# One of SyncE's three closing stores, split into four transfers over the DMA engines

## The chip, the cores and the metric

The kernel runs on one core of a Trainium2 chip. The metric is the device time of one execution in microseconds. Beside each timed kernel stands one profiled execution, whose trace gives the profile. A store or load is cut into rows, one row for each partition, and the rows are dealt out to the core's 16 DMA engines.

## The reference

The kernel computes the product of attention weights and values for 8 x 12 = 96 heads, all in float32:

```python
batch, n_heads, seq, head_dim = 8, 12, 1024, 64
np.einsum('bhqs,bhsd->bhqd', attn_weights, v)
```

The weights are 96 matrices of 1024 x 1024 (403 MB), v and the output 96 matrices of 1024 x 64 (25 MB each).

## The kernel before, in words

The heads are taken four at a time: NV = 24 groups q of four heads, each worked in two units, so NU = 48 units n. One unit's weights are loaded by GpSimd in one transfer (`load_attn`, lines 362 to 368), cast to bf16 on the way, into one of two buffers `abf`. TensorE transposes them in blocks against an identity (line 146), VectorE and ScalarE copy the transposed blocks from PSUM to `at` (line 302), TensorE multiplies them with the group's values `vbf` (line 207), the product goes to `ot` (line 310), is transposed back (line 192) and copied by ScalarE to the output buffer `osb` (line 283; the last unit's copy is shared with VectorE, line 343).

`osb` has five slots of two groups each; `slot(q)` gives the slot of group q. Two groups make 2 MB, 16 KiB in each of 128 partitions. Outputs are not stored when they are ready, but in bursts, since `osb` holds ten groups:

- behind the load for unit 18 GpSimd stores groups 0 to 7, behind that for unit 34 groups 8 and 9 and then 10 to 13 (`BURSTS`, lines 64 and 428 to 430);
- at the end of its program GpSimd stores groups 14 and 15, then 16 and 17 (lines 431 to 433; `HELD_FROM` = 14, `BY_SYNC` = 18), with `single_packet`;
- SyncE (SP) stores groups 18 and 19, then 20 and 21 (lines 458 and 459), and last 22 and 23 (lines 460 and 461).

What sets SP's order is its own program, lines 440 to 463. It passes on the landings of loads to TensorE (lines 445 to 456). The weights of the last two units (`HALVED` = 46 and on) come in two halves each, and line 455 waits for the second half of each. Only then does SP wait for the bursts (line 457, long true by then) and come to its stores, so that the first two are issued right behind the landing of the last load. `store` (lines 376 to 382) waits on `s_out`, which counts ScalarE's copies to `osb`, and issues one DMA that adds 16 to the semaphore `s_end` when it has landed, one from each DMA engine. The last store waits for the last copies through `s_vbf` (line 460).

The end of the program is ScalarE's wait on `s_end` (line 464) for the value that line 463 has put in a register: 16 for each of SP's stores, so 48. GpSimd's two last stores are waited for in line 357.

Of the kernel before, what the change touches and what calls it, by code (L numbers as in the profile page):

```python
# [10 lines left out]
def kernel(  # L11
# [18 lines left out]
    nc = tc.nc  # L30
# [5 lines left out]
    D = v.shape[-1]  # L36
    NH = B * H
    P = 128
    VH = 4
    VP = P // VH  # L40
    G = Q // VP // 2
# [8 lines left out]
    NV = NH // VH  # L50
# [4 lines left out]
    BY_SYNC = NV - 6  # L55
# [12 lines left out]
    def slot(q):  # L68
        return q % NO // 2
# [4 lines left out]
    def out_n(q, fours):  # L74
        return out_h[ds(q * VH, fours * VH)].rearrange(
            "(n eight) (p r) d -> (eight p) n (r d)", eight=V8, p=P // V8
        )
# [24 lines left out]
    osb = sb("osb", [P, NO // 2, 4 * G, D], fp32)  # L102
# [10 lines left out]
    s_v, s_osb, s_end, s_second = sem("s_v"), sem("s_osb"), sem("s_end"), sem("s_second")  # L113

    s_bank = [sem(f"s_bank{b}") for b in range(4)]
    s_ot, s_vbf, s_out = sem("s_ot"), sem("s_vbf"), sem("s_out")
# [21 lines left out]
    with tc.tile_critical(sync_engine=mybir.EngineType.Pool, no_gpsimd_drain=True):  # L138
# [237 lines left out]
        def store(q, fours, eng, done, ready=None):  # L376
            eng.wait_ge(s_out, ready or 2 * (q + fours) + 1)
            at_slot = osb[:, ds(slot(q), fours // 2)].rearrange("p n r d -> p n (r d)")
            eng.dma_start(  # L379
                out=out_n(q, fours), in_=at_slot,  # L380
                **({"single_packet": True} if eng is pool and fours == 2 else {}),
            ).then_inc(done, 16)

        def store_2(q):
            store(q, 2, pool, s_osb)

# [6 lines left out]
            out=ident,  # L393
            in_=ident,
# [8 lines left out]
            out=spread,  # L403
            in_=spread,
# [8 lines left out]
            out=spread_4,  # L413
            in_=spread_4,
# [6 lines left out]
        for n in range(NU - 2):  # L421
            q, i = n // 2, n % 2
# [9 lines left out]
        for q in range(HELD_FROM, BY_SYNC, 2):  # L432
            store_2(q)
# [11 lines left out]
        for k in range(1, NV // 2):  # L445
            stored = 2 * (k - 1)
            if stored in BURSTS:
                done = list(BURSTS).index(stored)
# [6 lines left out]
            nc.sync.wait_ge(*second_of(n))  # L455
            nc.sync.sem_inc(s_half)
        nc.sync.wait_ge(s_osb, 16 * sum(len(x) for x in BURSTS.values()))
        for q in range(BY_SYNC, NV - 2, 2):
            store(q, 2, nc.sync, s_end)
        nc.sync.wait_ge(s_vbf, NV * VH + 2)  # L460
        store(NV - 2, 2, nc.sync, s_end, NU)
        landed = nc.scalar.alloc_register("landed")
        nc.scalar.reg_mov(landed, 16 * (NV - BY_SYNC) // 2)
    tc.keep_in_program_order(nc.scalar.wait_ge(s_end, nc.scalar.snap(landed)))
    tc.keep_in_program_order(nc.scalar.sem_inc(s_end, 1))

# [29 lines left out]
```

## Time and profile before

| | |
|---|---|
| median of 3 runs | 1051.45 us (1051.25 to 1051.61) |
| the profiled execution | 1051.77 us |
| its span, first to last instruction | 1050.0 us |
| mean granted TensorE clock | 0.874 |
| TensorE busy | 792.7 us (75%) |
| VectorE / ScalarE busy | 389.9 us (37%) / 469.5 us (45%) |
| DMA packets and bytes moved | 10662, 239.68 MB |
| read from HBM / written to it | 427.82 MB / 25.17 MB |
| SP's stores issued at | 1024.9, 1025.3 and 1037.7 us |

Times in the trace are counted from the span's first instruction. "DMA" rows give the mean busy share of the 16 DMA engines in tenths, 9 for 90% or more, and GB/s what they moved, with a packet's bytes counted in the slice where it starts; in a window the 40 slices are as long as the window divided by 40. A queue's line gives its packets, megabytes, and the time that its packets took as a share of the time of 16 engines. q0 is GpSimd's queue of transfers, q1 SP's. Packets under 512 bytes are the completions by which a DMA engine tells that its share of a transfer is done, or other small ones. The packets carry no number of the DMA engine that moved them.

### The profile page before, as it was taken

Reading aid. Unit: us, or ns where it says so; the run is one execution under the profiler, and the core shown is the slowest. Engines: PE = TensorE matmul, PEld = TensorE weight load, DVE = VectorE, ACT = ScalarE, POOL = GpSimd, SP = SyncE. Lnnn points to the kernel's source line nnn. Section 1 sums busy time; section 2 is a strip of 40 time slices with the busy share of each in tenths; the row PEclk is TensorE's granted clock in tenths of the full one; section 3 lists DMA queues with packets and bytes.
Section 4 is the critical chain, followed back from the end, with each engine's and each line's share of the span. In section 5 each row is a group of like instructions: output and inputs, shape, how many; then the busy total and the mean of one; then the engine's idle time right before and its main releaser. Section 6 shows DMA issues by size and latency. Waiting matters only on the chain.

```text
span 1050.0 us, 17671 instructions
## 1 busy us (share of the span) xinstructions
PE 792.7 (75%) x7272; PEld 708.0 (67%) x7272; DVE 389.9 (37%) x585; ACT 469.5 (45%) x590; POOL 38.1 (4%) x69
## 2 busy tenths in 40 slices
PE   0777789489789493887949879859578794988984
PEld 0676678478678482777848678747567684878874
DVE  1443344235334251343424344324224341533542
ACT  0445355345445361344535455344335443545643
POOL 2000000000000000000000000000000000000100
PEclk9889789799898796889879989889879987889997
DMA  9999999999999999999999999999999999999998
GB/s 216 224 220 217 218 218 206 220 220 220 216 220 215 212 216 379 220 216 218 211 216 217 220 220 216 209 225 216 324 227 218 219 208 225 216 213 220 213 222 384
DMA packets 10662, 239.68 MB, mean 228 GB/s; under 512 B 1056, under 2 KB 1056, under 8 KB 1184
## 3 DMA queue, kind: packets, MB, share of 16 engines
q0 software_dynamic: 10080, 232.26, 98.8%
q1 hardware_dynamic: 576, 7.34, 1.7%
q8 instruction: 3, 0.05, 0.0%
q14 instruction: 3, 0.02, 0.0%
HBM read 427.82 MB, written 25.17 MB: 431 GB/s over the span
## 4 chain that ended last, share of the span: by engine, by line
DMA 71%; PE 26%; issue 1%; POOL 1%; ACT 0%; DVE 0%; ACTq 0%; SPq 0%; POOLq 0%
DMA abf<-in_attn_weights_dram 63%; PE bank L146 22%; DMA out_dram<-osb 8%; PE bank L163 2%; PE bank L207 1%; PE bank L192 0%; POOL vr L371 0%; ACT osb L283 0%; DVE osb L283 0%; ACT vbf L275 0%; PE bank L179 0%; POOL abf L365 0%; ACT ot L310 0%; POOL out_dram L379 0%; ACTq L283 0%
## 5 line engine op out<-in xcount | busy, mean ns | idle before, releaser
L146 PE MATMUL bank<-ident,abf 128*128 128x128 f32 x3072 | 432.3, 308 | 207.7 <-DMA abf<-in_attn_weights_dram 184.6
L146 PEld LDWEIGHTS bank<-ident,abf 128*128 128x128 f32 x3072 | 422.6, 212 | 219.3 <-DMA abf<-in_attn_weights_dram 192.1
L302 DVE COPY at<-bank 128x1024 bf16<-128x1024 bf16 x480 | 319.7, 688 | 399.7 <-PE bank L146 397.6
L302 ACT COPY at<-bank 128x1024 bf16<-128x1024 bf16 x288 | 287.9, 1012 | 327.2 <-PE bank L146 327.2
L207 PE MATMUL bank<-at,vbf 128*64 128x256 bf16 x3072 | 224.8, 285 | 0.0
L207 PEld LDWEIGHTS bank<-at,vbf 128*64 128x64 bf16 x3072 | 203.6, 111 | 20.1 <-issue 11.2
L283 ACT COPY osb<-bank 64x512 f32 (+1 forms) x194 | 112.4, 580 | 32.9 <-PE bank L192 30.3
L310 DVE COPY ot<-bank 128x512 f32<-128x512 f32 x48 | 33.2, 691 | 210.0 <-PE bank L207 210.0
L192 PE MATMUL bank<-ident,ot 128*128 128x128 f32 x392 | 61.3, 308 | 34.5 <-ACT vbf L275 26.3
L310 ACT COPY ot<-bank 128x512 f32<-128x512 f32 x48 | 28.1, 585 | 130.5 <-PE bank L207 130.5
L192 PEld LDWEIGHTS bank<-ident,ot 128*128 128x128 f32 x392 | 50.4, 157 | 46.6 <-ACT vbf L275 37.1
L163 PE MATMUL bank<-vr,spread 32*128 32x512 bf16 x704 | 79.8, 375 | 1.3 <-issue 0.9
L163 PEld LDWEIGHTS bank<-vr,spread 32*128 32x128 bf16 x704 | 32.7, 93 | 41.2 <-issue 4.1
L275 ACT CAST vbf<-bank 128x512 bf16<-128x512 f32 x48 | 25.8, 588 | 70.9 <-PE bank L163 69.5
L365 POOL DMA_DIRECT2D abf<-in_attn_weights_dram x50 | 26.9, 537 | 811.6 <-PE bank L146 810.8
L275 DVE CAST vbf<-bank 128x512 bf16<-128x512 f32 x48 | 30.9, 686 | 28.8 <-PE bank L163 28.0
L302 ACT ACT_TABLE_LOAD x12 | 15.4, 1283 | 6.1 <-DMA osb<-in_v_dram 5.9
L371 POOL DMA_DIRECT2D vr<-in_v_dram x6 | 4.0, 674 | 134.1 <-PE bank L163 112.6
L379 POOL DMA_DIRECT2D out_dram<-osb x5 | 3.1, 620 | 7.7 <-ACT osb L283 7.7
L283 DVE COPY osb<-bank 64x512 f32<-64x512 f32 x2 | 1.4, 690 | 3.0 <-PE bank L192 3.0
L345 DVE MEMSET ident<- 128x128 f32 x1 | 0.2, 165 | 5.9 <-DMA osb<-in_v_dram 5.9
L179 PE MATMUL bank<-vr,spread 32*128 32x512 bf16 x32 | 2.1, 377 | 0.1
(13 smaller groups left out, 9.9 us busy)
## 6 DMA issues: line engine op xcount, KB each, us to landing
abf<-in_attn_weights_dram POOLq DMA_DIRECT2D x46, 4096.0 KB, 29.1
vr<-in_v_dram POOLq DMA_DIRECT2D x5, 2048.0 KB, 15.2
out_dram<-osb POOLq DMA_DIRECT2D x1, 8192.0 KB, 40.2
abf<-in_attn_weights_dram POOLq DMA_DIRECT2D x4, 2048.0 KB, 24.6
out_dram<-osb POOLq DMA_DIRECT2D x3, 2048.0 KB, 35.4
out_dram<-osb SPq DMA_DIRECT2D x3, 2048.0 KB, 13.5
out_dram<-osb POOLq DMA_DIRECT2D x1, 4096.0 KB, 42.4
osb<-in_v_dram SPq DMA_DIRECT2D x1, 1024.0 KB, 4.8
```

What stands on the lines that cost most here:

```text
L146: last = pe.matmul(out=pt[g % 4][:, k], lhsT=words[:, k], rhs=ident, is_transpose=True, start=(k == 0), stop=(k == KW - 1),)
L163: last = pe.matmul(out=banks[h], lhsT=spread[rows, j, ds(VB - 1 - b, P)], rhs=vr[rows, n // 2, b], start=(b == 0), stop=(b == VB - 1),)
L179: last = pe.matmul(out=banks[h], lhsT=spread_4[rows, h, ds(VF - 1 - b, P)], rhs=vr[rows, 0, n * VF + b], start=(b == 0), stop=(b == VF - 1),)
L192: last = pe.matmul(out=px[j0 // 4][:, ds(j * P, P)], lhsT=ot[:, j0 + j], rhs=ident, is_transpose=True, start=(j == 0), stop=(j == 3),)
L207: last = pe.matmul(out=outs, lhsT=vbf[:, 2 * kw + par, h], rhs=at[:, ds(half * GH, GH), kw, ds(h * VP, VP), par], start=(n == 0), stop=(n ...
L275: copy(out=vbf[:, :, h], in_=ps.rearrange("p (k d) -> p k d", k=SB)).then_inc(s_vbf)
L283: last = copy(out=rows[ds(n // 2 % 2 * HP, HP), ds(pp * 2 * G + n % 2 * G, G)].rearrange("p (half j) d -> p j half d", half=2)[:, ds(4 * k ...
L302: copy(out=at[:, g].rearrange("c k j two -> c (k j two)"), in_=bank[g % 4].bitcast(bf16),).then_inc(s_bank[g % 4])
L310: copy(out=ot.rearrange("c j (pp h p) -> c h j pp p", pp=2, h=VH)[:, ds(2 * e, 2)], in_=po[e].rearrange("c (h j p pp) -> c h j pp p", h=2, ...
L365: pool.dma_start(out=abf[n % 2][:, ds(g0, gn)].rearrange("p g s -> p (g s)"), in_=attn_q[n // 2][:, ds((n % 2 * G + g0) * S, gn * S)],).th ...
L371: pool.dma_start(out=vr[:, ds(q % V_AT_ONCE // 2, fours // 2)].rearrange("p n b x -> p n (b x)"), in_=v_n(q, fours),).then_inc(s_v, 16)
L379: eng.dma_start(out=out_n(q, fours), in_=at_slot, **({"single_packet": True} if eng is pool and fours == 2 else {}),).then_inc(done, 16)
```

## The change

SP's first store, of groups 18 and 19, is issued as four transfers in place of one. Each row of 16 KiB is taken as two halves of 8 KiB. The first transfer moves the first half of all 128 partitions; the other three move the second half of partitions 0 to 79, 80 to 115 and 116 to 127. By the words of the change that deals 17 half rows to each of DMA engines 0 to 11 and 13 to each of 12 to 15, where each had 16: 8 + 5 + 3 + 1 and 8 + 5. The wait ahead of the store stays the same. SP's second and third store stay as they were, and the value that the program's end waits for becomes 16 x 6 = 96, since six transfers now add to `s_end`.

```diff
+        def store_uneven(q, eng, done):
+            eng.wait_ge(s_out, 2 * (q + 2) + 1)
+            half = 2 * G * D
+            for p0, pn, x0 in ((0, P, 0), (0, 80, half), (80, 36, half), (116, 12, half)):
+                eng.dma_start(
+                    out=out_n(q, 2)[ds(p0, pn), 0, ds(x0, half)],
+                    in_=osb[ds(p0, pn), slot(q)].rearrange("p r d -> p (r d)")[:, ds(x0, half)],
+                ).then_inc(done, 16)
...
-        for q in range(BY_SYNC, NV - 2, 2):
+        store_uneven(BY_SYNC, nc.sync, s_end)
+        for q in range(BY_SYNC + 2, NV - 2, 2):
             store(q, 2, nc.sync, s_end)
         nc.sync.wait_ge(s_vbf, NV * VH + 2)
         store(NV - 2, 2, nc.sync, s_end, NU)
         landed = nc.scalar.alloc_register("landed")
-        nc.scalar.reg_mov(landed, 16 * (NV - BY_SYNC) // 2)
+        nc.scalar.reg_mov(landed, 16 * ((NV - BY_SYNC) // 2 + 3))
```

## The prediction

> **What bounds the kernel now.** I read the page's head first, then the end of the chain of waits, then the DMA view of the last 30 us in ever smaller windows, and last the issues of SyncE (SP).
>
> ```profile
> span 1050.0 us, 17671 instructions
> DMA  9999999999999999999999999999999999999998
> DMA 71%; PE 26%; issue 1%; POOL 1%; ACT 0%; DVE 0%; ACTq 0%; SPq 0%; POOLq 0%
> out_dram<-osb SPq DMA_DIRECT2D x3, 2048.0 KB, 13.5
> ```
>
> The 16 DMA engines are busy in every slice, and the chain is mostly DMA. The change touches one of three 2 MB stores that SP issues at the end, so only the tail matters. The chain cannot show that tail: its last piece is a copy that ends at 1037.7, because the chain starts from the last instruction of a computing engine, and the last wait of the program is for a landing.
>
> ```profile
> 1037.02 0.69 DVE osb L283
> L465 ACTq EVENT_SEMAPHORE  x1: 17/17/17, 1049.1 to 1049.1; - x1
> ```
>
> So 11.4 us pass between the last copy and the moment ScalarE's wait (line 464) is over. What fills them is in the windows (the last two numbers of a row are the DMA share and GB/s):
>
> ```profile
> 1025.00:1030.00 5.00, 5.00 (x43) 4.82 (x42) 4.19 (x7) 4.12 (x5) 0.00 (x0) 1.00 1.03 439
> 1040.00:1045.00 5.00, 0.00 (x0) 0.00 (x0) 0.00 (x0) 0.00 (x0) 0.00 (x0) 0.50 1.02 436
> 1045.00:1050.00 5.00, 0.00 (x0) 0.00 (x0) 0.00 (x0) 0.00 (x0) 0.00 (x0) 0.50 0.44 187
> ```
>
> All 16 engines move stores at 436 GB/s with no gap until about 1046. No issue, no copy and no semaphore is late there; what ends the program is the engine with most left to do. The window from 1040 to 1046 gives the price of a row, and the one from 1047 to 1049 (40 slices of 0.05 us) shows which engines end last:
>
> ```profile
> DMA packets 176, 2.59 MB, mean 431 GB/s; under 512 B 18, under 2 KB 18, under 8 KB 18
> q1 hardware_dynamic: 174, 2.59, 100.8%
> ...
> GB/s 0 328 328 0 0 0 328 0 0 0 328 0 0 328 0 0 0 0 328 0 0 0 328 0 0 0 0 0 0 0 0 0 0 0 0 0 0 0 0 0
> DMA packets 19, 0.11 MB, mean 57 GB/s; under 512 B 12, under 2 KB 12, under 8 KB 12
> ```
>
> Of 176 packets 158 are rows of 16 KiB (18 are completions), and 100.8% of 16 engines for 6 us is 96.8 us: **0.61 us a row**. In the last window 12 of the 16 engines still have their completion to come, and 328 marks one row that starts in that slice. Seven rows start: at about 1047.07, 1047.12, 1047.32, 1047.52, 1047.67, 1047.92 and 1048.12. Rows of one engine follow each other by 0.61, so 1047.07 and 1047.67, 1047.32 and 1047.92, 1047.52 and 1048.12 are three engines with two rows each; 1047.12 is the last row of a fourth. So **three engines are late**: they end at 1048.28, 1048.53 and 1048.73, the fourth at 1047.73, and the other twelve earlier (the last rows that start before 1047 do so near 1046.94, in the next fence, so they end by 1047.55). From the last end to the landing at 1049.1 are another 0.37, and to the span's end 0.9.
>
> ```profile
> GB/s 1311 0 0 0 655 0 655 655 1311 0 655 655 1966 655 0 0 0 0 655 655 0 0 0 0 1966 0 0 0 655 0 0 656 1311 0 0 0 655 1311 0 0
> DMA packets 29, 0.41 MB, mean 410 GB/s; under 512 B 4, under 2 KB 4, under 8 KB 4
> ```
>
> (Window 1046 to 1047: slices of 0.025 us, 655 is one row.)
>
> **The change part by part.** It replaces one store of 128 rows of 16 KiB, 8 rows to an engine, by four of 8 KiB rows: 128 rows (8 to an engine), 80 (5), 36 on twelve engines (3) and 12 on twelve (1). If it does that, an engine of 0 to 11 moves 17 half rows where it moved 16, and one of 12 to 15 moves 13.
>
> *The rows.* A half row by bytes is 0.61 / 2 = 0.305 us. The twelve get 1 x 0.305 = +0.31, the four get 3 x 0.305 = -0.92. The profile does not name a packet's engine. If the three late ones are among 12 to 15 and the fourth is not, the late ones end at 1048.73 - 0.92 = 1047.81 and the fourth at 1047.73 + 0.31 = 1048.04: the end comes from 1048.73 to 1048.04, **-0.7 us**. If the fourth is in the group too, the next engine ends at 1047.55 + 0.31 = 1047.86: -0.87. If a late engine is one of 0 to 11, its end moves out: up to +0.31.
>
> *The price of an 8 KiB row.* The nearest rows are those of the first load of v, 128 rows of 8 KiB by the same queue, in the first 6 us:
>
> ```profile
> DMA packets 160, 1.57 MB, mean 262 GB/s; under 512 B 16, under 2 KB 16, under 8 KB 16
> ...
> q1 hardware_dynamic: 144, 1.05, 49.4%
> ```
>
> 49.4% of 16 x 6 us is 47.4 us for 128 rows: 0.37 us, with each engine's first access in it. So a half row lies between 0.305 and 0.37, and 17 of them cost 0 to 17 x 0.065 = 1.1 us more than by bytes. I take 0.305, as rows in the tail follow one another without a gap (100.8%); the other end would turn -0.7 into +0.4.
>
> *Issues and the queue behind them.* The change adds three DMA issues on SP, ahead of the store of line 459's second pass and of the last store. An issue takes 0.33 to 0.57 us:
>
> ```profile
> L379 SPq DMA_DIRECT2D out_dram<-osb x3: 332/342/567, 1024.9 to 1037.7; - x3
> 1024.88 0.96 SPq L379 DMA_DIRECT2D out_dram<-osb  x2
> 1037.74 0.33 SPq L379 DMA_DIRECT2D out_dram<-osb  x1
> q0 software_dynamic: 117, 1.70, 99.8%
> ```
>
> The second store would be issued at about 1025.3 + 3 x 0.34 = 1026.3, at worst 1027.0. That costs nothing: from 1024 to 1028 (last row) the engines move only GpSimd's stores, at 99.8%, and each engine then has 17 half rows of the first store to move before the second is wanted. Without that cover it would cost 1.0 us. The last store is issued when the copies are done (1037.7), long after SP is free again. Nothing but SP waits behind these issues; the new count in line 463 is a constant.
>
> *Turns with GpSimd's second store.* From 1028 to 1036 the engines serve both queues:
>
> ```profile
> q1 hardware_dynamic: 108, 1.77, 51.7%
> q0 software_dynamic: 111, 1.72, 50.4%
> ```
>
> That is about row for row. With half rows on SP's side GpSimd's store would end earlier and SP's later; an engine's sum of bytes is the same, so nothing is gained or lost, and nobody waits for GpSimd's store but ScalarE, which waits longer for SP's. Three more completions per engine are 4 bytes each; before, they leave no gap between the stores.
>
> The sum: -0.7 (rows), 0 (half rows), 0 (issues), 0 (turns). The profiled execution took 1051.77 us with a span of 1050.0 and would take 1051.07; it lies 0.3 above the median of 1051.45. By the median: **1050.8 us**, a gain of 0.07%. A run of this kernel can tell about 0.2% (2.1 us) from no change, so this forecast counts as "the same", and no version of it counts as faster: with all lag gone the last engine could end at best with the twelve, 1.2 us sooner.
>
> **The rivals.** *Wrong engines.* The late three may not be among 12 to 15; the profile shows no numbers of engines. Then the change does its split and the end moves by +0.3, to 1051.8. What made them late bears on it only weakly: queue q8 has three 16 KiB instruction packets, the first in the window 38 to 39 and the last in 55 to 56, each of nearly 1 us (6% of 16 us):
>
> ```profile
> q8 instruction: 3, 0.05, 0.0%
> q8 instruction: 1, 0.02, 6.1%
> q8 instruction: 1, 0.02, 6.0%
> ```
>
> That is one for each late engine, perhaps, and a queue that never runs dry carries such a lag to the end. Which engines carried them is not told. [...] Also here belongs that the split is not the one named.
>
> *Shared partitions: slower.* In every transfer of this trace an engine's rows come from a full set of 128 partitions, and two queues interleave at 436 GB/s (windows above), so no engine disturbs another. In the pieces of 80, 36 and 12 rows the rows per engine are another number, so engines must read partitions that other engines read before. If two engines that read neighbouring partitions halve each other's rate, the 5 + 3 + 1 = 9 half rows of an engine cost 9 x 0.305 = 2.7 us more, and with three or four on one place 5.5 to 8.2. Place: the nine half rows behind the first piece, from about 1027.7 + 8 x (0.61 + 0.305) = 1035 to 1038 (the first piece's turns with GpSimd's store come before), with every engine full, so that each delay goes to the end. It decides against the change as soon as these rows average over 0.305 + 0.7 / 9 = 0.38 us, and beyond 0.2% when they cost 2.8 us, about double. Double gives 1051.45 + 2.7 - 0.7 = 1053.5, or 1054.2 if the balance is lost with it; the worst is 1059. For it: an 8 KiB row did take 0.37 on average once. Against it: no row here shows two engines in each other's way. [...]
>
> **How the numbers follow.** Balance as reckoned (1050.5 to 1051.2): 0.42. Wrong engines or no effect (1051.3 to 1051.9): 0.12. Shared partitions: 0.44, of it 0.05 within 0.2% (under 1053.6), 0.27 from there to 1055.5 and 0.12 above. Something that saves more than 2.1 us: 0.02. So faster 0.02, the same 0.42 + 0.12 + 0.05 = 0.59, slower 0.39. The range from 1050.5 to 1055.5 leaves out the 0.12 above and a few hundredths below; the upper half row price (+0.4) lies within. The likeliest case is the first, 1050.8.
>
> **What would show it.** Right: in the last 2 us no three engines stand alone with two rows each; the completion of the last store comes at most 1.2 us after the first, SP's queue keeps 100% of 16 engines to 1046, and the landing is near 1048.4. Wrong engines: the same picture with rows that start up to 1048.4. Shared partitions: between 1034 and 1039 the DMA rate falls well below 436 GB/s while queue q1 still shows 100% (rows that take longer), and the landing is past 1051. Wrong in another way: a gap in the DMA share after 1028, which would mean that SP's four issues are late.

## The result, and the profile after

The changed kernel takes 1054.33 us (median of 12 runs, 1053.23 to 1055.04) against 1051.47 for the kernel before (12 runs, 1050.99 to 1052.28): 2.9 us slower, a ratio of 1.0025 with a 95% interval of 1.0016 to 1.0034. The forecast was 1050.8. The profiled execution took 1054.60 us with a span of 1052.8.

First the lines of the page and of SP's issues that answer to those shown of the kernel before:

```profile
span 1052.8 us, 17674 instructions
DMA  9999999999999999999999999999999999999998
```

```profile
1024.41 2.17 SPq L388 DMA_DIRECT2D out_dram<-osb  x4
1026.63 10.81 SPq L379 DMA_DIRECT2D out_dram<-osb  x2
```

```profile
L475 ACTq EVENT_SEMAPHORE  x1: 17/17/17, 1051.9 to 1051.9; - x1
```

The page shows nothing: its slices are 26 us wide. SP issues its four transfers from 1024.4 to 1026.6 and the second store at 1026.6, as reckoned, and the last landing moves from 1049.1 to 1051.9, 2.8 us, which is the whole loss. Where it arises is in the windows of one us (last two numbers: DMA share and GB/s; a row's time counts where it starts, so a share over 1 means rows that last into the next window):

```profile
1034.00:1035.00 1.00, 0.47 (x4) 0.47 (x5) 0.00 (x0) 0.47 (x1) 0.00 (x0) 1.00 1.01 426
1036.00:1037.00 1.00, 0.00 (x0) 0.00 (x0) 0.99 (x2) 0.39 (x1) 0.00 (x0) 1.00 1.03 393
1037.00:1038.00 1.00, 0.00 (x0) 0.00 (x0) 0.05 (x1) 0.00 (x0) 0.00 (x0) 0.55 1.83 262
1038.00:1039.00 1.00, 0.00 (x0) 0.00 (x0) 0.00 (x0) 0.00 (x0) 0.00 (x0) 0.50 1.04 164
1039.00:1040.00 1.00, 0.00 (x0) 0.00 (x0) 0.00 (x0) 0.00 (x0) 0.00 (x0) 0.50 0.39 139
1040.00:1041.00 1.00, 0.00 (x0) 0.00 (x0) 0.00 (x0) 0.00 (x0) 0.00 (x0) 0.50 0.80 262
1041.00:1042.00 1.00, 0.00 (x0) 0.00 (x0) 0.00 (x0) 0.00 (x0) 0.00 (x0) 0.50 1.01 426
```

From 1037 to 1041 the engines move 262, 164, 139 and 262 GB/s where 430 was moved from 1030 to 1034. What is missing, 168 + 266 + 291 + 168 = 893 GB/s for one us each, is 0.89 MB, or 2.1 us at 430. The engines are not idle meanwhile. The DMA view from 1037 to 1040:

```profile
DMA packets 66, 0.57 MB, mean 188 GB/s; under 512 B 16, under 2 KB 16, under 8 KB 16
q1 hardware_dynamic: 66, 0.57, 108.7%
```

50 rows take 108.7% of 16 x 3 us, 1.04 us each, at a mean size of 11 KB. At 0.61 us for 16 KiB they would take 0.42. Row by row in the trace, 31 of the 50 are half rows with a mean of 1.25 us, and 19 are rows of 16 KiB of the next store with a mean of 0.70. So rows got slower; none came late. The rest of the loss is the spread of the ends. In the window from 1047 to 1052 (slices of 0.125 us) all 16 completions lie behind 1047, where before four had come, and rows still start 3.9 us into the window:

```profile
GB/s 262 262 655 393 393 131 393 655 262 262 0 524 655 131 262 0 524 524 262 131 0 393 393 131 0 0 262 262 131 0 0 131 0 0 0 0 0 0 0 0
DMA packets 80, 1.05 MB, mean 210 GB/s; under 512 B 16, under 2 KB 16, under 8 KB 16
```

### The profile page after: what moved, and what is told of

Same layout as the page of the kernel before. It is cut to its first block, busy times and chain, and to the rows that moved or that the text cites. A ratio compares the mean times of both kernels' runs of the same rounds, so it can differ in the third digit from the quotient of the medians.

```text
span 1052.8 us, 17674 instructions
## 1 busy us (share of the span) xinstructions
PE 792.7 (75%) x7272; PEld 706.3 (67%) x7272; DVE 390.1 (37%) x585; ACT 469.5 (45%) x590; POOL 38.1 (4%) x69
## 4 chain that ended last, share of the span: by engine, by line
DMA 71%; PE 25%; issue 1%; POOL 1%; ACT 0%; DVE 0%; ACTq 0%; SPq 0%; POOLq 0%
DMA abf<-in_attn_weights_dram 63%; PE bank L146 22%; DMA out_dram<-osb 8%; PE bank L163 2%; PE bank L207 1%; PE bank L192 0%; POOL vr L371 0%; ACT osb L283 0%; DVE osb L283 0%; ACT vbf L275 0%; PE bank L179 0%; POOL abf L365 0%; ACT ot L310 0%; POOL out_dram L379 0%; ACTq L283 0%
## 5 line engine op out<-in xcount | busy, mean ns | idle before, releaser
L207 PE MATMUL bank<-at,vbf 128*64 128x256 bf16 x3072 | 228.1, 288 | 0.1
```

The source lines that it names most:

```text
L207: last = pe.matmul(out=outs, lhsT=vbf[:, 2 * kw + par, h], rhs=at[:, ds(half * GH, GH), kw, ds(h * VP, VP), par], start=(n == 0), stop=(n ...
```

## The experiments

The theory now is the prediction's second rival, called P in the expectations: rows that different DMA engines read at the same time from the same few partitions share one rate. Its rivals: K, a transfer on twelve engines is slow in itself; R, what is slow is writing few neighbouring rows of the output; F, half rows and more transfers cost by themselves. The diffs below are shortened to the edit that matters; the count that the end of the program waits for follows the number of transfers.

**Half rows alone.** The pieces in line 387 become (0, 128, 0) and (0, 128, half):

```diff
-            for p0, pn, x0 in ((0, P, 0), (0, 80, half), (80, 36, half), (116, 12, half)):
+            for p0, pn, x0 in ((0, P, 0), (0, P, half)):
```

> SyncE's first store is split by columns alone: two transfers of 128 half rows each, 16 half rows for every DMA engine. The changed kernel was 2.9 us slower than before (1054.33 against 1051.47), and its DMA rate fell to 262, 164, 139 and 262 GB/s in the four us from 1037 to 1041. Theory P (half rows of the narrow pieces meet on the same partitions): this kernel has no narrow piece, so no dip and 1051.3 to 1051.8. Rival K (a transfer on twelve DMA engines is slow in itself): the same, no dip. Rival F (half rows and more transfers cost by themselves): it has half of the half rows' cost and one more transfer in place of three, so 1052.4 to 1053.

Measured: 1051.51 us against 1051.53, ratio 1.0000 (0.9991 to 1.0009). Its DMA view from 1037 to 1040:

```profile
DMA packets 117, 1.35 MB, mean 451 GB/s; under 512 B 16, under 2 KB 16, under 8 KB 16
q1 hardware_dynamic: 117, 1.35, 105.7%
```

Nearly the same engine time (105.7% here, 108.7% in the changed kernel) moves 1.35 MB here and 0.57 MB there. Row by row in the traces, the first 128 half rows to start take 39.7 us together in both kernels; the other 128 take 39.6 us here and 72.3 us in the changed kernel, 0.31 and 0.56 us each. That half rows cost by themselves is ruled out.

**Uneven pieces, even loads.** Both pieces on 16 engines, 16 half rows for each:

```diff
-            for p0, pn, x0 in ((0, P, 0), (0, 80, half), (80, 36, half), (116, 12, half)):
+            for p0, pn, x0 in ((0, P, 0), (0, 80, half), (80, 48, half)):
```

> The second halves go in pieces of 80 and 48 partitions, both on 16 DMA engines: 8 + 5 + 3 = 16 half rows for each engine, no engine is relieved, no transfer uses twelve engines. [...] Rival K: no dip, 1051.3 to 1051.8. Rival R (few neighbouring rows of the output in HBM are what is slow): a dip for the 48 rows, smaller than for 12, 1051.5 to 1053. Rival F: 1053 to 1054.

Measured: 1052.34 against 1051.53, ratio 1.0009 (1.0000 to 1.0018), between 1051.68 and 1053.60. The window from 1036 to 1039 has 360 GB/s:

```profile
DMA packets 139, 1.08 MB, mean 360 GB/s; under 512 B 32, under 2 KB 32, under 8 KB 32
```

The run with two halves moves 442 GB/s in the same window, the changed kernel 273. So there is a shallow dip with no transfer on twelve engines, which speaks against K as the whole cause; but the interval begins at 1.0000, and the time alone would not decide it. P and R stand.

**The same transfers from other partitions.** The pieces of 36 and 12 read every third and every tenth partition and write the rows that they wrote; those 48 half rows get other rows' values:

```diff
-            for p0, pn, x0 in ((0, P, 0), (0, 80, half), (80, 36, half), (116, 12, half)):
+            for p0, pn, step, r0, x0 in (
+                (0, P, 1, 0, 0), (0, 80, 1, 0, half), (0, 36, 3, 80, half), (0, 12, 10, 116, half),
+            ):
-                    out=out_n(q, 2)[ds(p0, pn), 0, ds(x0, half)],
-                    in_=osb[ds(p0, pn), slot(q)].rearrange("p r d -> p (r d)")[:, ds(x0, half)],
+                    out=out_n(q, 2)[ds(r0, pn, 1), 0, ds(x0, half)],
+                    in_=osb[ds(p0, pn, step), slot(q)].rearrange("p r d -> p (r d)")[:, ds(x0, half)],
```

> The four transfers of the changed kernel in number, size, DMA engines and output rows, but the pieces of 36 and 12 read their half rows from partitions 0, 3, 6 ... 105 and 0, 10, 20 ... 110 instead of 80 to 115 and 116 to 127 (so 48 half rows of the output get other rows' values). Theory P: the dip from 1037 to 1041 is gone and what is left is the moved rows: 1050.5 to 1051.5. Rivals K, R and F: all that they blame is still there, 1053.8 to 1054.8 with the dip.

Measured: 1053.33 against 1051.53, ratio 1.0016 (1.0007 to 1.0025). That is no theory's number: a us below the changed kernel, and its runs spread from 1051.40 to 1054.62. P's range is missed by nearly 2 us. The profile is of the execution of 1051.40 us, the fastest, and shows hardly a dip (418 GB/s from 1036 to 1039):

```profile
DMA packets 160, 1.25 MB, mean 418 GB/s; under 512 B 43, under 2 KB 43, under 8 KB 43
```

So the same transfers on the same engines can run nearly without the dip. What the slower executions, the other ten of eleven, look like this profile does not say. The piece of 80 still reads partitions 0 to 79 here, and the two moved pieces now read among them too. The same kernel once more:

> The kernel with the changed kernel's four transfers read from partitions three and ten apart, once more, for a second profile: its runs lay between 1051.40 and 1054.62 and the profile was of the fastest. Theory P: a slow execution shows the same picture as the changed kernel, some rows of 8 and 16 KiB that take 1.2 us or more and a dip in the DMA rate between 1036 and 1041, because the twelve meet by chance of timing; a fast one shows none. If a slow one shows no dip, something else differs between executions.

Measured: one run, 1051.95 us, with 399 GB/s from 1036 to 1039: a little of a dip in an execution near the lower end of that spread. This leaves it open: no execution of 1053 us and more was profiled.

**The same balance from strided pieces.** The whole output again, 17 and 13 half rows; the diff is against the kernel just above:

```diff
-                (0, P, 1, 0, 0), (0, 80, 1, 0, half), (0, 36, 3, 80, half), (0, 12, 10, 116, half),
+                (0, P, 1, 0, 0), (96, 32, 1, 96, half), (0, 48, 2, 0, half),
+                (1, 12, 8, 1, half), (3, 12, 8, 3, half), (5, 12, 8, 5, half), (7, 12, 8, 7, half),
-                    out=out_n(q, 2)[ds(r0, pn, 1), 0, ds(x0, half)],
+                    out=out_n(q, 2)[ds(r0, pn, step), 0, ds(x0, half)],
```

> The same 17 and 13 half rows for the DMA engines, and the whole output right, but in seven transfers: 128 first halves; second halves of partitions 96 to 127 (2 rows an engine), 0, 2 ... 94 (3 rows), and four pieces of twelve partitions eight apart (1, 9 ... 89 and so on, 1 row an engine on twelve engines). [...] Rival K: four transfers on twelve engines in place of two, 1055 to 1057. Rival R: output rows are spread too, 1050.7 to 1052. Rival F: six more transfers in place of three, 1056 to 1058.

Measured: 1052.74 against 1051.53, ratio 1.0013 (1.0004 to 1.0022), from 1051.83 to 1054.75. Four transfers on twelve engines cost less than the changed kernel's two, and seven less than four: K and F foretold 1055 to 1058. But it does not reach the kernel before, and lies 0.7 us above the range that R gave.

**Source and destination apart.** These four enlarge the effect. Two transfers of 128 half rows as in the first experiment, and behind them four extra transfers of twelve half rows, 1.2 us of bytes for engines 0 to 11. They write over rows of groups 0, 2, 4 and 6, which end up wrong. In the diff `p0`, `step`, `r0` and `rstep` stand for the numbers of each kernel.

```diff
+            for old in range(0, 8, 2):
+                eng.dma_start(
+                    out=out_n(old, 2)[ds(r0, 12, rstep), 0, ds(half, half)],
+                    in_=osb[ds(p0, 12, step), slot(q)].rearrange("p r d -> p (r d)")[:, ds(half, half)],
+                ).then_inc(done, 16)
```

> Both halves of SyncE's first store go as two transfers of 128 half rows (that alone gave 1051.51 against 1051.53), and behind them come four extra transfers of twelve half rows, which write over output rows of groups 0, 2, 4 and 6 that were stored long before (so those rows end up wrong; the work is extra). Here the twelve are read from partitions 116 to 127 and written to output rows 116 to 127. By bytes alone engines 0 to 11 get 4 x 0.305 = 1.2 us more: 1051.8 if the late engines are among 12 to 15, 1052.7 if they are not. [...] Rival K (a transfer on twelve engines is slow in itself) and rival R (few neighbouring output rows): slow too, two to four times the changed kernel's 2.9 us, 1057 to 1062.

> As the first of this set, but the twelve half rows are read from partitions 0, 10 ... 110 and written to output rows 0, 10 ... 110. [...] Rival R: 1051.8 to 1052.7, by bytes. Rival K: as slow as the first, 1057 to 1062.

> Read from partitions 116 to 127, written to output rows 0, 10 ... 110. Theory P: as slow as the first of the set, 1056 to 1058. Rival R: by bytes, 1051.8 to 1052.7. Rival K: 1057 to 1062.

> Read from partitions 0, 10 ... 110, written to output rows 116 to 127. Theory P: as fast as the second of the set, 1052 to 1054. Rival R: as slow as the first, 1056 or more. Rival K: 1057 to 1062.

| read from partitions | written to output rows | us (before 1051.47) | ratio, 95% interval |
|---|---|---|---|
| 116 to 127 | 116 to 127 | 1058.66 | 1.0067, 1.0051 to 1.0084 |
| 116 to 127 | 0, 10 ... 110 | 1058.45 | 1.0066, 1.0049 to 1.0083 |
| 0, 10 ... 110 | 116 to 127 | 1052.92 | 1.0017, 1.0007 to 1.0026 |
| 0, 10 ... 110 | 0, 10 ... 110 | 1052.51 | 1.0013, 1.0004 to 1.0023 |

Read down the table: the partitions that are read decide (7 us or 1.0 to 1.5), the output rows do not. R falls, and so does K, whose transfers are the same in all four. P is left, though both kernels with near partitions lie above its 1056 to 1058. Its two ranges for the table were the author's estimates from how many of the extra rows meet in one place, which no run shows. Twelve neighbours were tried at 116 to 127 alone: that neighbours elsewhere are as slow was not tested. The wide transfers of the run with two halves read these same partitions at the usual 0.31 us a row, so they are not slow in themselves. The windows of the first and last kernel of the table:

```profile
1038.00:1040.00 2.00, 0.00 (x0) 0.00 (x0) 0.00 (x0) 0.00 (x0) 0.00 (x0) 0.50 1.09 143
1040.00:1042.00 2.00, 0.00 (x0) 0.00 (x0) 0.00 (x0) 0.00 (x0) 0.00 (x0) 0.50 1.03 115
1042.00:1044.00 2.00, 0.00 (x0) 0.00 (x0) 0.00 (x0) 0.00 (x0) 0.00 (x0) 0.50 1.05 119
```

```profile
1038.00:1040.00 2.00, 0.00 (x0) 0.00 (x0) 0.00 (x0) 0.00 (x0) 0.00 (x0) 0.50 1.09 455
1040.00:1042.00 2.00, 0.00 (x0) 0.00 (x0) 0.00 (x0) 0.00 (x0) 0.00 (x0) 0.50 0.99 426
```

All engines stay busy in both (shares about 1), at 115 or 426 GB/s. An engine that moves 16 KiB in 0.61 us moves 26.9 GB/s, so the 115 and 119 of the first kernel are, by an estimate from these numbers, what 4.3 to 4.4 engines move at that price. Row by row in the trace, the extra 8 KiB rows there take 2.37 us, nearly eight times 0.305, and the 16 KiB rows beside them 1.18, about twice their 0.61. The trace names neither the engine nor the partitions of a row, so how the rate is shared it does not show.

**The same twelve rows behind the last store.** The near rows of the first line of the table, issued behind the last store:

```diff
         store_uneven(BY_SYNC, nc.sync, s_end)
-        extra_rows(BY_SYNC, nc.sync, s_end)
...
         store(NV - 2, 2, nc.sync, s_end, NU)
+        extra_rows(BY_SYNC, nc.sync, s_end)
```

> [...] If narrow rows are slow whatever the others do: 4 x 2.37 = 9.5 us, 1059 to 1061.

Measured: 1054.82 against 1051.55, ratio 1.0032 (1.0020 to 1.0044). From 1049 to 1051:

```profile
DMA packets 35, 0.12 MB, mean 61 GB/s; under 512 B 20, under 2 KB 20, under 8 KB 20
q1 hardware_dynamic: 35, 0.12, 52.5%
```

15 half rows take 52.5% of 16 x 2 us, 1.12 us each (1.26 for the typical one), about half of the 2.37 that the same rows took behind the first store. So what these rows cost changed with what ran beside them: 1059 to 1061, for rows that are slow whatever the others do, is missed by 4 us. The first of the extra rows, which start near 1047, take only 0.31.

**Which engines are late.** The extra rows of the table's last line, read from v in HBM:

```diff
-                    in_=osb[ds(0, 12, 10), slot(q)].rearrange("p r d -> p (r d)")[:, ds(half, half)],
+                    in_=v_n(old, 2)[ds(0, 12, 10), 0, ds(half, half)],
```

> Which engines are late? Four extra transfers of twelve half rows behind SyncE's first store, as in the set before, but read from v in HBM and written to output rows 0, 10 ... 110 of groups 0, 2, 4 and 6 (which end up wrong; the work is extra): engines 0 to 11 get four rows of 8 KiB more and nothing is read from SBUF for them. If a row costs 0.31 us as usual: with the late three among 12 to 15 the twelve come up to them and the end hardly moves, 1051.5 to 1051.9, and in the last two us the completions lie close together; with a late engine among 0 to 11 the end moves by the whole 1.2 us, 1052.6 to 1052.9, and the late ones still stand alone. If rows from HBM to HBM cost more, the same two cases with that price.

Measured: 1052.52 against 1051.55, ratio 1.0009 (1.0000 to 1.0018), by its size alone nearer to "a late engine among 0 to 11". The profiled execution (1052.24 us) says otherwise:

```profile
1024.79 0.90 SPq L391 DMA_DIRECT2D out_dram<-osb  x2
```

```profile
L487 ACTq EVENT_SEMAPHORE  x1: 17/17/17, 1049.6 to 1049.6; - x1
```

```profile
GB/s 1638 0 0 328 655 655 0 0 655 328 655 328 1311 0 0 0 983 328 328 0 328 328 655 0 0 0 0 0 0 328 0 0 0 0 0 0 0 0 0 0
DMA packets 45, 0.49 MB, mean 246 GB/s; under 512 B 15, under 2 KB 15, under 8 KB 15
```

SP's first issue, which follows the slowest engine's last load, is at 1024.79 against 1024.88 before. With 1.2 us of extra rows that engine would have landed its last row at 1049.1 - 0.1 + 1.2 = 1050.2; the landing is at 1049.6. And in the window from 1047 to 1049 15 of 16 completions are still to come where there were 12: the twelve have come up to the late ones. The completion packets settle it. In the kernel before, the last completion of 15 of the 16 engines follows their completion of the last load by 24.32 us, that of one by 25.07. Here that time is 25.61 us for eleven engines, 26.35 for one, and 24.37 for four, which are therefore the four without extra rows. These four are the latest of the last load (1023.27, 1023.68, 1023.80 and 1024.35), and their last completions come at 1047.63, 1048.04, 1048.17 and 1048.72. In this execution, then, the late three are among the four that the change calls 12 to 15. The engine of 26.35 us is one of the twelve and the last to end, 0.3 us behind all others; why it needs 0.7 us more than the other eleven (as one of the 16 did in the kernel before), and why the median of the runs lies 1.0 us above the kernel before, is not explained.

**The twelve rows alone.** The changed kernel with only its last piece read from partitions ten apart (its twelve half rows get other rows' values); the diff is against the kernel with both pieces moved:

```diff
-                (0, P, 1, 0, 0), (0, 80, 1, 0, half), (0, 36, 3, 80, half), (0, 12, 10, 116, half),
+                (0, P, 1, 0, 0), (0, 80, 1, 0, half), (80, 36, 1, 80, half), (0, 12, 10, 116, half),
```

> The changed kernel with its piece of 36 as it is (partitions 80 to 115) and only the piece of twelve read from partitions 0, 10 ... 110 in place of 116 to 127 (so twelve half rows of the output get other rows' values). Theory P: four pieces of twelve from partitions 116 to 127 cost 7.1 us in the earlier run, so one costs about 1.8; without it 1054.3 - 1.8 = 1052.5, between 1052 and 1053.2, and the dip between 1037 and 1041 is much shallower. If the piece of 36 is what costs: 1053.8 to 1054.6 with the dip.

Measured: 1053.91 against 1051.87, ratio 1.0020 (1.0010 to 1.0029), from 1052.42 to 1055.36: 2.0 us slower than before in place of 2.9. In the profiled execution (1052.65 us) the dip is shallower, with 303 and 311 GB/s:

```profile
1037.00:1038.00 1.00, 0.00 (x0) 0.00 (x0) 0.00 (x0) 0.00 (x0) 0.00 (x0) 1.00 1.21 303
1038.00:1039.00 1.00, 0.00 (x0) 0.00 (x0) 0.00 (x0) 0.00 (x0) 0.00 (x0) 0.79 0.87 311
```

The expected 1052.5 is missed. By the medians the piece of twelve is 0.8 us of the loss, not 1.8, which would leave the larger part to the pieces of 80 and 36. But the intervals of this kernel and the changed one overlap, and the twelve rows are now read where the piece of 80 reads too, so the division is not shown.

## Why the prediction was wrong, point by point

- **What bounds the tail**: right as far as it went. All engines were busy to the end, with three late ones; the run with rows from HBM puts those among 12 to 15 in its profiled execution.
- **The rows, -0.7 us**: this is the step that failed. It gave each half row 0.305 us wherever it was read, as if time belonged to the engine alone. In the changed kernel the later 128 of the store's half rows took 0.56 us on average, against 0.31 in the run with two halves and above the 0.38 from which the prediction itself turned against the change. That the partitions that are read make rows slow is what the table shows: with the same sizes and counts, 7 us with partitions 116 to 127 and 1.0 to 1.5 with partitions ten apart. The sum also left out that the change moves rows to other engines and none to other partitions: the second halves of 80 to 127 are still read from 80 to 127.
- **The price of an 8 KiB row, 0.305 to 0.37**: right for what it measured (two transfers of 128 half rows cost -0.02 us), but the bound came from a transfer of 128 partitions and did not hold for the pieces of 80, 36 and 12 (0.56 us on average). The upper end of +0.4 was therefore far too low.
- **Issues and turns, 0**: right. SP's three more issues were covered: the DMA share is 1.01 and the rate 426 GB/s from 1034 to 1035, before the dip. The run with two halves shows no cost of turns (1051.51 us against 1051.53).
- **Wrong engines, +0.3**: not the cause. The late three were among 12 to 15 in the one execution where they could be told, that of the run with rows from HBM. In the changed kernel SP's six transfers give 88 completions, 4 x 16 and 2 x 12, so the pieces of 36 and 12 did go to twelve engines each.
- **Shared partitions, 1053.5 to 1054.2**: the case that came nearest, at 1054.3. That engines on neighbouring partitions halve each other's rate was the author's assumption: the runs show that the partitions that are read decide, not how a rate is shared. The place was named, 1035 to 1038; the dip came at 1037 to 1041, behind rows still at the usual rate. The price of "double" was near the total by chance: single rows went up to 3.2 us, others kept 0.31, and in the table's first kernel an extra row took 2.37 us, nearly eight times its usual 0.305, not twice. With 0.44 it was the largest single case, and the forecast of 1050.8 came from taking the price of the nearest row for an access that no row showed.

Open: why runs of the kernels with spread partitions differ by 3 us from one execution to the next and why spreading the pieces of 36 and 12 took only 1.0 of the 2.9 us away; how the loss divides between the pieces of 80, 36 and 12 (no run spreads the piece of 80 alone); which engines and partitions slow each other, which no run maps; and 0.5 us of the run with rows from HBM. No kernel here is faster than the one before.

## What to carry to other kernels

Here a tail that kept all DMA engines busy depended on the partitions that were read as well as on the engines' shares of the rows: four extra transfers of twelve half rows cost 7 us from partitions 116 to 127 and 1.0 to 1.5 from partitions ten apart. Read the DMA share and the GB/s of a window together: the share of 1.04 at 164 GB/s from 1038 to 1039, where 430 was moved before, meant that rows got slow, not that work came late. And when an access has no row in the trace, the price of the nearest row is no estimate of it; let the range and the likeliest case follow the mechanism that would make it different.

## What the runs showed of the hardware

With four extra transfers of twelve half rows from partitions 116 to 127 behind SP's first store, these 8 KiB rows took 2.37 us in place of 0.305, and rows of 16 KiB beside them 1.18 in place of 0.61; behind the last store the extra rows took 1.26 us. Where the rows were written in HBM made no difference that the runs could tell (1058.66 and 1058.45; 1052.51 and 1052.92).
